# RWKV-7 recurrence: the solve of the triangle as a step of its own two units ahead, and inner products on quarters of the array

## Chip, cores and metric

The kernel runs on one core of one Trainium2 chip. The metric is the device time of one execution in microseconds; several runs are taken, and their median counts. Engines are called PE (TensorE), PEld (its weight loads), DVE (VectorE), ACT (ScalarE), POOL (GpSimd) and SP (SyncE, which here only issues DMAs).

## What is computed

A decoder trunk for 1024 tokens of width 1024: one layer with an RWKV-7 time mix and an MLP, then one layer with sliding-window attention and an MLP. What matters here is the time mix. After projections of the shifted input (r, k, v, decay w, rate a, gate g), a recurrence runs over the tokens for 16 heads of width 64, each with a 64x64 state S:

```python
def step(S, inp):
    r_t, w_t, k_t, v_t, a_t, b_t = inp
    sa = jnp.einsum('bhvk,bhk->bhv', S, a_t)
    S = S * w_t[:, :, None, :] + sa[..., None] * b_t[:, :, None, :] + v_t[..., None] * k_t[:, :, None, :]
    y = jnp.einsum('bhvk,bhk->bhv', S, r_t)
    return S, y
...
y = wkv7(rh, wh, kh, vh, -kk, kk * ah)
```

Then each head's y is normalised, a bonus term is added, the gate is applied, and an output product follows. All inputs and the output are float32.

## The kernel before

**Chunks and units.** The recurrence is not run token by token. Tokens go in chunks of L = 64. Inside a chunk the step is a triangular system: with the products of b and k with a and r (64x64 per head, masked), a unit lower triangle is inverted, and everything else is matrix products. A *unit* is 128 tokens (NC = 2 chunks) of 8 heads (GH; GP = 4 pairs of heads, one head of a pair on partitions 0 to 63, the other on 64 to 127). There are 16 units, in order of time, two groups of heads for each block of tokens.

**Steps of a unit.**
- `prep` (L574) loads `ld` (r, k, w, a of the unit, written by the projections to HBM), and makes RA (r and a, scaled), bk (b and k, scaled), EL (the chunk's decay) and bonus.
- `inner` (L627) multiplies bk by RA: for each of 8 (pair, chunk) and each half `hp` one product with K = 64, 128 columns and N = 128 (L642), four per PSUM tile and half. Of the result a quarter is copied to XT (ACT, L646), and two parts go through a mask to AR (L647) and RT (L648) on DVE. The diagonal 32x32 blocks of the triangle are stored to HBM (dXs, L659, issued on ACT's queue) and loaded as Xs with one block per partition (L661, SP). bk is transposed to BK (L665, L666).
- `solve` (L669) inverts the 32x32 blocks on POOL, 31 steps of two instructions (L680, L682) on TT, stores TT (dTT, L684), clears a block of RT with a memset on POOL (L687) and loads the inverse into RT (L689). The store and the loads are on SP's queue.
- `join` (L693) joins two 32x32 inverses to one of 64x64: a transpose on DVE (L700), two sets of small matmuls (L705, L711), copies on ACT (L707, L713).
- `chunks` (L716) runs the two chunks one after the other: L743, L745 (ACT), L748, L749, L752 (with RT, the inverse), L754 (DVE), L757, L759, L762 (DVE: the state for the second chunk, in SV), L763, L766, L767. bv is loaded and multiplied on POOL (L732).
- `finish` (L770) normalises y: L781 and L787 on PE, the power -1/2 on POOL (L791), `spread` (L563: the copy `wide` on ACT, L568, transposes L570), the gate, and the store of z.

**Order.** The Tile framework builds each engine's queue ahead of time: it walks the instructions by priority in a simulated time and puts each one on its engine's queue as soon as, in that time, its inputs and buffers are there. On the chip each engine works its queue in that order and waits where an input is late. `urgent` (L93) gives the recurrence one stream of priorities ahead of all else, in the order of the program. `recurrence` (L804) sets that order by strings: ORDER2 = 'cispfj' means chunks(n), inner(n+1), solve(n+1), prep(n+2), finish(n), join(n+1); ORDER0 and ORDER1 stand at the borders of the parts. The projections are made in three parts of 256, 256 and 512 tokens, so units 0 to 3, 4 to 7 and 8 to 15 need part 0, 1 and 2.

**Beside it.** Units 0 to 7 run beside the projections; then come the output product of the first 512 tokens (`mix_out`) and its MLP, beside which units 8 to 15 run. Projections and MLP split every weight and activation into two float32r halves, hi and lo: casts on ACT (L129), subtractions on DVE (L130), three matmuls each on PE (L134 to L136), weights loaded by SP (L269).

PSUM has pools `big` (4 banks: products), `sm` (2: prep and inner) and `sq` (2, `turn()`: join, chunks, finish).

Of the kernel before, what the change touches and what calls it, by code (L numbers as in the profile page):

```python
# [50 lines left out]


ORDER0 = 'cfipsj'
ORDER1 = 'cifpsj'
ORDER2 = 'cispfj'
# [19 lines left out]
class Trunk:  # L75
# [487 lines left out]
    def spread(self, src, ps):  # L563
# [3 lines left out]
        w = self.t(self.rp, "wide", [P, n, 2, D])  # L567
# [59 lines left out]
    def inner(self, prepared):  # L627
# [4 lines left out]
        AR = t("AR", [P, 2, GP * NC, 2 * L], 2)  # L632
        BK = t("BK", [P, GP * NC, 2, D], 2)
        RT = t("RT", [P, 2, GP * NC, L], 2)
# [15 lines left out]
        for hp in range(2):  # L650
            hs = self.sides(hp)[0]
            nc.sync.dma_start(AR[hs, hp], RA[hs])

# [6 lines left out]
        for js in range(JS):  # L660
            nc.sync.dma_start(Xs[js * 2 * NQ:(js + 1) * 2 * NQ], dX.rearrange("b h q k i -> (b h q) k i"))  # L661
        for r0 in range(0, GP, 2):
# [4 lines left out]
        return AR, BK, RT, EL, bonus, XT, Xs  # L667

    def solve(self, made):  # L669
# [3 lines left out]
        AR, BK, RT, EL, bonus, XT, Xs = made  # L673
# [11 lines left out]
        for hp in range(2):  # L685
# [5 lines left out]
        return made  # L691

    def join(self, made):  # L693

        nc = self.nc
        AR, BK, RT, EL, bonus, XT, Xs = made
# [12 lines left out]
        for q in range(n):  # L709
            for hp, b, k in sides:  # L710
                nc.tensor.matmul(ps[k:k + B, q], AT[k + B:k + L, q], RT[k + B:k + L, hp, q, B:], start=True, stop=True)  # L711
        for hp, b, k in sides:
            nc.scalar.copy(RT[k:k + B, hp, :, B:], ps[k:k + B, 0:n])  # L713
        return AR, BK, RT, EL, bonus

    def chunks(self, blk, g, made):  # L716
# [15 lines left out]
        nc.gpsimd.tensor_tensor(bv[L:], bv[L:], bonus[L:].unsqueeze(3).broadcast_to([L, NC, GH, D]), ALU.mult)  # L732
# [6 lines left out]
        for c in range(NC):  # L739
# [11 lines left out]
            for pi, hp, bs, ks in heads:  # L751
                nc.tensor.matmul(ps[bs, pi], RT[ks, hp, pi * NC + c], pb[ks, pi], start=True, stop=True)  # L752
# [5 lines left out]
            sn = t("sn", [P, GP, D])  # L758
# [360 lines left out]
```

## Time and profile before

| what | us |
|---|---|
| median of 3 runs (2684.1 to 2687.0) | 2686.05 |
| the profiled execution | 2683.85 |
| its span on the core | 2682.1 |
| PE busy in the span | 2549.6 |
| DVE busy | 1688.0 |
| ACT busy | 1289.1 |
| POOL busy | 616.9 |
| mean granted clock of PE, as a share of 2.4 GHz | 0.974 |

The profile is of one execution. Busy times are the time in which an engine had an instruction under way; matmuls are pipelined, so PE's busy time is not time at its peak. A clock below 1 means that for part of the stretch the lower of two levels was granted. In the profile L-numbers are lines of the kernel, "x16" is a count, "<-" names the tile written and those read, and in brackets stands how long the engine was idle before and who released it.

### The profile page before, as it was taken

Reading aid. Unit: us, or ns where it says so; the run is one execution under the profiler, and the core shown is the slowest. Engines: PE = TensorE matmul, PEld = TensorE weight load, DVE = VectorE, ACT = ScalarE, POOL = GpSimd, SP = SyncE. Lnnn points to the kernel's source line nnn. Section 1 sums busy time; section 2 is a strip of 40 time slices with the busy share of each in tenths; the row PEclk is TensorE's granted clock in tenths of the full one; section 3 lists DMA queues with packets and bytes.
Section 4 is the critical chain, followed back from the end, with each engine's and each line's share of the span. In section 5 each row is a group of like instructions: output and inputs, shape, how many; then the busy total and the mean of one; then the engine's idle time right before and its main releaser. Section 6 shows DMA issues by size and latency. Waiting matters only on the chain.

```text
span 2682.1 us, 43180 instructions
## 1 busy us (share of the span) xinstructions
PE 2549.6 (95%) x15226; PEld 2066.2 (77%) x15226; DVE 1688.0 (63%) x3204; ACT 1289.1 (48%) x2670; POOL 616.9 (23%) x1213
## 2 busy tenths in 40 slices
PE   7978988998889999999999999999999999999999
PEld 5867766765767777778888888888888888888887
DVE  8678788665766666545467876445899544444444
ACT  5555566455444434334455555334666433434342
POOL 6276643741464444410010000001000000000000
PEclk9988989999889999999999999999999999999999
DMA  5756644654634444333434444342446332423332
GB/s 178 203 171 171 181 115 121 181 145 148 178 101 117 121 117 117 109 103 119 142 94 150 123 129 146 92 154 90 136 142 204 114 102 91 125 91 102 98 98 96
DMA packets 440633, 349.62 MB, mean 130 GB/s; under 512 B 97105, under 2 KB 360417, under 8 KB 440417
## 3 DMA queue, kind: packets, MB, share of 16 engines
q1 hardware_dynamic: 423008, 344.77, 42.5%
q10 hardware_dynamic: 17408, 2.10, 0.5%
q8 instruction: 120, 1.97, 0.3%
q14 instruction: 97, 0.79, 0.1%
HBM read 280.71 MB, written 57.67 MB: 126 GB/s over the span
## 4 chain that ended last, share of the span: by engine, by line
PE 54%; DVE 2%; DMA 0%; ACT 0%; issue 0%; POOL 0%; DVEq 0%; ACTq 0%; POOLq 0%
PE big L134 17%; PE big L135 17%; PE big L136 17%; PE sm L134 1%; PE sm L135 0%; PE sm L136 0%; PE sq L956 0%; PE sq L957 0%; PE big L252 0%; DVE sc L962 0%; DVE wl L130 0%; DVE m2k L260 0%; PE sq L933 0%; DMA wr<-in_b_wq 0%; DVE b L1038 0%; DVE st L966 0%
## 5 line engine op out<-in xcount | busy, mean ns | idle before, releaser
L129 ACT CAST wh<-wr 128x512 fp32r<-128x512 f32 x741 | 458.2, 620 | 872.4 <-PE big L136 457.5
L130 DVE TENSOR_TENSOR wl<-wr,wh 128x512 fp32r<-128x512 f32 x741 | 529.4, 718 | 485.5 <-issue 226.0
L135 PE MATMUL big<-wl,m2k 128*128 128x512 f32 (+1 forms) x1472 | 580.6, 395 | 7.2 <-DVE wl L130 5.4
L134 PE MATMUL big<-m2k,wh 128*128 128x512 f32 (+3 forms) x1528 | 576.4, 380 | 9.8 <-ACT m2k L129 4.8
L136 PE MATMUL big<-m2k,wl 128*128 128x512 f32 (+2 forms) x1528 | 571.3, 376 | 7.4 <-DVE wl L130 7.3
L135 PE MATMUL big<-m2k,wh 128*128 128x512 f32 (+2 forms) x1528 | 571.1, 375 | 7.3 <-POOL m2k L130 4.2
L136 PE MATMUL big<-wh,m2k 128*128 128x512 f32 (+1 forms) x1472 | 567.5, 392 | 2.8 <-POOL m2k L130 2.8
L134 PE MATMUL big<-wh,m2k 128*128 128x512 f32 (+1 forms) x1472 | 515.9, 395 | 9.8 <-ACT m2k L129 7.5
L134 PEld LDWEIGHTS big<-m2k,wh 128*128 128x128 f32 (+1 forms) x1528 | 290.3, 190 | 70.8 <-ACT m2k L129 6.9
L136 PEld LDWEIGHTS big<-m2k,wl 128*128 128x128 f32 (+1 forms) x1528 | 290.8, 191 | 59.6 <-DVE wl L130 10.1
L134 PEld LDWEIGHTS big<-wh,m2k 128*128 128x128 f32 x1472 | 281.3, 192 | 71.1 <-ACT m2k L129 9.2
L135 PEld LDWEIGHTS big<-m2k,wh 128*128 128x128 f32 (+1 forms) x1528 | 290.6, 190 | 58.5 <-POOL m2k L130 6.7
L135 PEld LDWEIGHTS big<-wl,m2k 128*128 128x128 f32 x1472 | 282.1, 192 | 69.2 <-DVE wl L130 10.4
L136 PEld LDWEIGHTS big<-wh,m2k 128*128 128x128 f32 x1472 | 281.2, 191 | 59.3 <-POOL m2k L130 3.3
L680 POOL TENSOR_TENSOR tmp<-Xs,TT 128x60 f32<-128x60 f32 (+24 forms) x496 | 193.6, 390 | 142.0 <-DMA Xs<-dXs 105.4
L130 DVE TENSOR_TENSOR m2k<-relu,m2k 128x512 fp32r<-128x512 f32 (+1 forms) x200 | 137.0, 687 | 122.7 <-ACT m2k L129 122.0
L682 POOL TENSOR_TENSOR TT<-TT,tmp 128x60 f32<-128x60 f32 (+24 forms) x496 | 199.1, 401 | 37.8
L129 ACT CAST m2k<-relu 128x512 fp32r<-128x512 f32 (+1 forms) x272 | 146.4, 544 | 46.3 <-DVE relu L353 33.8
L322 DVE TENSOR_TENSOR b<-b,big 128x512 f32<-128x512 f32 x192 | 124.8, 681 | 10.2 <-PE big L136 9.7
L223 POOL TENSOR_TENSOR ss<-ss,mhalf 128x4 f32<-128x4 f32 (+1 forms) x10 | 8.9, 888 | 488.7 <-DVE ss L222 488.7
L223 POOL TENSOR_TENSOR qn<-qn,mhalf 128x8 f32<-128x8 f32 x16 | 26.7, 1671 | 399.3 <-DVE qn L222 346.0
L314 ACT ACTIVATE relu<-relu 128x512 f32<-128x512 f32 x128 | 80.8, 632 | 3.5
(229 smaller groups left out, 3089.7 us busy)
## 6 DMA issues: line engine op xcount, KB each, us to landing
wr<-in_mlp_w SPq DMA_DIRECT2D x512, 256.0 KB, 2.7
wr<-in_a_w_rkv SPq DMA_DIRECT2D x144, 256.0 KB, 3.1
ld<-dP SPq DMA_DIRECT2D x16, 1024.0 KB, 7.7
dS<-sc SPq DMA_DIRECT2D x28, 512.0 KB, 2.9
row<-dS SPq DMA_DIRECT2D x112, 128.0 KB, 2.8
dP<-stg SPq DMA_DIRECT2D x64, 128.0 KB, 2.8
AR<-RA SPq DMA_DIRECT2D x32, 256.0 KB, 4.5
Xs<-dXs SPq DMA_DIRECT2D x64, 128.0 KB, 2.7
```

Source lines behind the costliest of these rows:

```text
L129: self.nc.scalar.copy(hi, src)
L130: (engine or self.nc.vector).tensor_tensor(lo, src, hi.bitcast(F32), ALU.subtract)
L134: mm(ps, ah, bh, start=start, stop=False)
L135: mm(ps, ah, bl, start=False, stop=False)
L136: mm(ps, al, bh, start=False, stop=stop)
L223: nc.gpsimd.tensor_tensor(dst, dst, self.mhalf[:, :n], ALU.pow)
L314: nc.scalar.activation(r, r, AF.Square)
L322: nc.vector.tensor_tensor(v, v, ps[tt], ALU.add)
L680: nc.gpsimd.tensor_tensor(v, Xs[:, k:k + 1, k + 1:].broadcast_to([P, m, n]), TT[:, 0:m, k:k + 1].broadcast_to([P, m, n]), ALU.mult)
L682: nc.gpsimd.tensor_tensor(TT[:, 0:m, k + 1:], TT[:, 0:m, k + 1:], v, ALU.add)
```

## The change

The triangle of the inner products (b with a, the quarter that is solved) is made in a function of its own, `triangle`, which also stores and loads the blocks and runs `solve`, up to the store of dTT. `recurrence` calls it with `prep` in `begin(n + 3)`, after finish(n); `inner(n + 2)` stands before finish(n), and `join(n + 1)` before that. `inner` makes the remaining products, with 64 columns each: one set with N = 64 for RT (one mask instruction over 128 partitions instead of four over 64) and one with N = 128 for AR. RT's second half now holds the inverse for both halves of the heads. The memset and the loads of the inverse move from `solve` to `join`. Three short POOL instructions (memset, bv, the power) get a priority ahead of the stream. `finish` uses buffers of its own for the gate and the spread; `sn` shares pb's buffer and AT lies in XT.

```diff
-ORDER0 = 'cfipsj'
-ORDER1 = 'cifpsj'
-ORDER2 = 'cispfj'
...
-    def urgent(self, stream):
+    def urgent(self, stream, rank=1):
-        at = self.ahead.get(stream, -URGENT)
+        at = self.ahead.get(stream, -rank * URGENT)
...
-    def inner(self, prepared):
+    def triangle(self, prepared):
...
-        n = 2 * NC
-        for r0 in range(0, GP * NC, n):
-            pg = [self.small().rearrange("p (i m) -> p i m", i=n) for _ in range(2)]
-            for i in range(n):
-                for hp in range(2):
-                    hs = self.sides(hp)[0]
-                    nc.tensor.matmul(pg[hp][:, i], bk[hs, r0 + i], RA[hs, r0 + i], start=True, stop=True)
+        ps = self.small().rearrange("p (i m) -> p i m", m=L)
+        for i in range(GP * NC):
             for hp in range(2):
                 hs, bs, ks = self.sides(hp)
-                to = slice(r0, r0 + n)
-                nc.scalar.copy(XT[bs, to], pg[hp][bs, :, L:])
-                nc.vector.tensor_tensor(AR[ks, hp, to], pg[hp][ks], self.maskg[ks].unsqueeze(1).broadcast_to([L, n, 2 * L]), ALU.mult)
-                nc.vector.tensor_tensor(RT[bs, hp, to], pg[hp][bs, :, 0:L], self.maskg[bs, 0:L].unsqueeze(1).broadcast_to([L, n, L]),
-                                        ALU.mult)
...
+                nc.tensor.matmul(ps[bs, i], bk[hs, i, bs], RA[hs, i, L:], start=True, stop=True)
+        nc.scalar.copy(XT, ps)
...
+        return XT, self.solve(Xs)
+
+    def inner(self, prepared, tri):
...
+        for hp in range(2):
+            hs = self.sides(hp)[0]
+            nc.sync.dma_start(AR[hs, hp], RA[hs])
+        ps = self.small().rearrange("p (i m) -> p i m", m=L)
+        for i in range(GP * NC):
+            for hp in range(2):
+                hs, bs, ks = self.sides(hp)
+                nc.tensor.matmul(ps[bs, i], bk[hs, i, bs], RA[hs, i, 0:L], start=True, stop=True)
+        nc.vector.tensor_tensor(RT[:, 0], ps, self.maskg[:, 0:L].unsqueeze(1).broadcast_to([P, GP * NC, L]), ALU.mult)
+        n = GP * NC // 2
+        for r0 in (0, n):
+            ps = self.small().rearrange("p (i m) -> p i m", i=n)
+            for i in range(n):
+                for hp in range(2):
+                    hs, bs, ks = self.sides(hp)
+                    nc.tensor.matmul(ps[ks, i], bk[hs, r0 + i, ks], RA[hs, r0 + i], start=True, stop=True)
+            for hp in range(2):
+                ks = self.sides(hp)[2]
+                nc.vector.tensor_tensor(AR[ks, hp, r0:r0 + n], ps[ks], self.maskg[ks].unsqueeze(1).broadcast_to([L, n, 2 * L]), ALU.mult)
...
+    def join(self, made):
...
         for hp in range(2):
             r = self.sides(hp)[2].start
-            nc.gpsimd.memset(RT[r + B:r + L, hp, :, 0:B], 0.0)
+            with self.urgent("pool", 2):
+                nc.gpsimd.memset(RT[r + B:r + L, 1, :, 0:B], 0.0)
             for b in range(2):
-                nc.sync.dma_start(RT[r + b * B:r + (b + 1) * B, hp, :, b * B:(b + 1) * B],
+                nc.sync.dma_start(RT[r + b * B:r + (b + 1) * B, 1, :, b * B:(b + 1) * B],
                                   dT[:, :, b, hp].rearrange("j s q i -> (j s) q i"))
...
-            nc.vector.transpose(XT[b:b + B, :, 0:B], RT[k:k + B, hp, :, 0:B])
-        AT = self.t(self.rp, "AT", [P, n, B], F32)
+            nc.vector.transpose(XT[b:b + B, :, 0:B], RT[k:k + B, 1, :, 0:B])
+
+        AT = XT[:, :, 0:B]
...
+        with self.urgent("pool", 2):
+            nc.gpsimd.tensor_tensor(bv[L:], bv[L:], bonus[L:].unsqueeze(3).broadcast_to([L, NC, GH, D]), ALU.mult)
...
-            sn = t("sn", [P, GP, D])
+            sn = t("pb", [P, GP, D])
...
-        gt = t("m1", [P, GP, TB])
+        gt = t("gt", [P, GP, TB])
...
-        nc.gpsimd.tensor_tensor(r2, r2, self.mhalf[:, :GH], ALU.pow)
-        nc.vector.tensor_tensor(z2, z2, self.spread(rs, self.turn()), ALU.mult)
+        with self.urgent("pool", 2):
+            nc.gpsimd.tensor_tensor(r2, r2, self.mhalf[:, :GH], ALU.pow)
+        nc.vector.tensor_tensor(z2, z2, self.spread(rs, self.turn(), "wide2"), ALU.mult)
...
+        def begin(m):
+            if m < len(units):
+                ready[m] = self.prep(*units[m])
+                tri[m] = self.triangle(ready[m])
+
+        def inner(m):
+            if m < len(units):
+                made[m] = self.inner(ready.pop(m), tri.pop(m))
+
         with self.urgent("rec"):
-            made = self.inner(self.prep(*units[0]))
-            ready = self.prep(*units[1])
-            made = self.join(self.solve(made))
...
+            begin(0)
+            inner(0)
+            begin(1)
+            joined = self.join(made.pop(0))
+            inner(1)
+            begin(2)
         for n, u in enumerate(units):
             with self.urgent("rec"):
...
+                y, bv = self.chunks(*u, joined)
+                if n + 1 < len(units):
+                    joined = self.join(made.pop(n + 1))
+                inner(n + 2)
+                self.finish(*u, y, bv)
+                begin(n + 3)
             yield
```

## Rows read from the trace of the kernel before

**Rows 1.** Page, busy time of each engine: us (share of the span) xinstructions.
```profile
PE 2549.6 (95%) x15226; PEld 2066.2 (77%) x15226; DVE 1688.0 (63%) x3204; ACT 1289.1 (48%) x2670; POOL 616.9 (23%) x1213
```

**Rows 2.** Busy time by stage: stretch, length, engines, PE's granted clock, DMA share, GB/s.
```profile
120.00:700.00 580.00, 510.01 (x4151) 394.60 (x4150) 419.40 (x829) 326.20 (x723) 288.45 (x574) 0.93 0.54 158
700.00:820.00 120.00, 108.05 (x821) 87.92 (x822) 86.13 (x160) 48.60 (x95) 72.79 (x180) 0.86 0.43 118
820.00:1160.00 340.00, 324.83 (x2560) 258.26 (x2561) 215.55 (x396) 135.61 (x264) 150.67 (x349) 0.98 0.41 112
...
1260.00:2682.00 1422.00, 1411.24 (x6498) 1169.83 (x6496) 828.93 (x1577) 669.12 (x1359) 40.72 (x32) 1.00 0.39 121
```

**Rows 3.** Waits of DVE, 120 to 1260 us: in total, times, longest.
```profile
DVE XT L700 <- DMA RT<-dTT: 80.1, 17, 8.2
```

**Rows 4.** Timeline, 1019 to 1030 us: start, us, engine, line [idle before, releaser].
```profile
1021.95 0.38 SPq L684 DMA_DIRECT2D dTT<-TT  x1
...
1026.34 0.43 DVE L700 STREAM_TRANSPOSE XT<-RT 32x256 f32<-32x256 f32 x1 [7.51 <-DMA RT<-dTT]
...
1027.32 1.42 PE L743 MATMUL sq<-SV,AR 128*64 128x64 f32 x15 [3.19 <-issue]
```

**Rows 5.** Timeline of POOL in the MLP stage.
```profile
975.06 0.65 POOL L687 MEMSET RT<- 32x256 f32 x2 [17.10 <-PE sq L766]
987.92 2.14 POOL L791 TENSOR_TENSOR rs<-rs,mhalf 128x8 f32<-128x8 f32 x1 [12.21 <-DVE rs L790]
...
1041.41 0.65 POOL L687 MEMSET RT<- 32x256 f32 x2 [16.66 <-PE sq L766]
```

**Rows 6.** Groups by line, whole span: busy us, mean ns | idle before.
```profile
L682 POOL TENSOR_TENSOR TT<-TT,tmp 128x60 f32<-128x60 f32 (+24 forms) x496 | 199.1, 401 | 37.8
L680 POOL TENSOR_TENSOR tmp<-Xs,TT 128x60 f32<-128x60 f32 (+24 forms) x496 | 193.6, 390 | 142.0 <-DMA Xs<-dXs 105.4
```

**Rows 7.** Stretches round the waits of L700: two, then sums of ten and six.
```profile
423.00:439.00 16.00, 11.05 (x113) 8.31 (x111) 13.28 (x31) 10.03 (x22) 1.85 (x6) 0.89 0.52 154
...
741.00:757.00 16.00, 11.59 (x76) 9.33 (x75) 7.66 (x15) 1.97 (x4) 7.99 (x25) 0.69 0.52 133
...
886.00:902.00 16.00, 13.69 (x95) 10.67 (x92) 9.14 (x18) 4.68 (x9) 2.44 (x10) 0.89 0.39 99
...
sum 160.00, PE 135.92 PEld 105.84 DVE 103.98 ACT 77.02 POOL 45.88; mean PE 13.59 PEld 10.58 DVE 10.40 ACT 7.70 POOL 4.59
...
sum 96.00, PE 81.53 PEld 63.35 DVE 51.94 ACT 24.64 POOL 15.61; mean PE 13.59 PEld 10.56 DVE 8.66 ACT 4.11 POOL 2.60
```

**Rows 8.** Waits of PE: in total, times, longest.
```profile
PE sq L743 <- issue: 12.8, 6, 3.2
...
PE sq L705 <- DVE XT L700: 8.9, 3, 4.4
```

**Rows 9.** PE's products: chain that ended last, PE's timeline, group of L642.
```profile
1163.21 0.61 PE sq L752 x16
...
1173.00 0.86 PE sq L781 x2
...
946.64 1.16 PE L642 MATMUL sm<-RA,bk 64*128 64x128 f32 x16
947.74 0.50 PE L136 MATMUL big<-m2k,wl 128*128 128x512 f32 x1
...
L642 PE MATMUL sm<-RA,bk 64*128 64x128 f32 x512 | 56.5, 293 | 6.7 <-DVE RT L648 4.8 <-ACT wh L129 1.8
```

**Rows 10.** Groups by line on DVE and ACT.
```profile
L322 DVE TENSOR_TENSOR b<-b,big 128x512 f32<-128x512 f32 x192 | 124.8, 681 | 10.2 <-PE big L136 9.7
...
L648 DVE TENSOR_TENSOR RT<-sm,maskg 64x256 f32<-64x256 f32 x64 | 27.0, 422 | 1.1
...
L646 ACT COPY XT<-sm 64x256 f32<-64x256 f32 x64 | 23.4, 366 | 28.6 <-PE sm L642 26.3 <-PE sq L748 0.9 <-ACT XT L646 0.8
...
L666 ACT COPY BK<-sm 128x512 f32<-128x512 f32 x32 | 18.1, 588 | 5.8 <-PE sm L665 5.8
```

**Rows 11.** Waits of SP's queue, 820 to 1160 us.
```profile
SPq L684 <- POOL TT L682: 51.1, 6, 10.1
```

**Rows 12.** Waits of ACT.
```profile
ACT wide L568 <- POOL rs L791: 24.8, 12, 5.8
```

More of the change, by code (lines that the diff above doesn't have):

```diff
@@ L561, in project, with spread @@
         return nxt, self.gate_out(pt)
-    def spread(self, src, ps):
+    def spread(self, src, ps, tag="wide"):
         nc = self.nc
         n = src.shape[1]
-        w = self.t(self.rp, "wide", [P, n, 2, D])
+        w = self.t(self.rp, tag, [P, n, 2, D])
         nc.scalar.copy(w, src.unsqueeze(3).broadcast_to([P, n, 2, D]))
@@ L661, in inner @@
             nc.sync.dma_start(Xs[js * 2 * NQ:(js + 1) * 2 * NQ], dX.rearrange("b h q k i -> (b h q) k i"))
+        return XT, self.solve(Xs)
+    def inner(self, prepared, tri):
+        nc = self.nc
+        t = lambda tag, shape, bufs=1, dt=F32: self.t(self.rp, tag, shape, dt, bufs)
+        RA, bk, EL, bonus = prepared
+        AR = t("AR", [P, 2, GP * NC, 2 * L], 2)
+        BK = t("BK", [P, GP * NC, 2, D], 2)
+        RT = t("RT", [P, 2, GP * NC, L], 2)
+        for hp in range(2):
[17 more added lines that the diff above has]
+                nc.vector.tensor_tensor(AR[ks, hp, r0:r0 + n], ps[ks], self.maskg[ks].unsqueeze(1).broadcast_to([L, n, 2 * L]), ALU.mult)
         for r0 in range(0, GP, 2):
@@ L666, in inner, with solve @@
             nc.scalar.copy(BK[:, r0 * NC:(r0 + 2) * NC].rearrange("p i h d -> p (i h d)"), ps.rearrange("p i m -> p (i m)"))
-        return AR, BK, RT, EL, bonus, XT, Xs
-    def solve(self, made):
+        return AR, BK, RT, EL, bonus, *tri
+    def solve(self, Xs):
         nc = self.nc
         t = lambda tag, shape, bufs=1, dt=F32: self.t(self.rp, tag, shape, dt, bufs)
-        AR, BK, RT, EL, bonus, XT, Xs = made
         TT = t("TT", [P, B // JS, B])
@@ L684, in solve @@
         nc.sync.dma_start(dT.rearrange("j s b h q i -> (s b h q) j i"), TT)
+        return dT
+    def join(self, made):
+        nc = self.nc
+        AR, BK, RT, EL, bonus, XT, dT = made
         for hp in range(2):
             r = self.sides(hp)[2].start
-            nc.gpsimd.memset(RT[r + B:r + L, hp, :, 0:B], 0.0)
+            with self.urgent("pool", 2):
+                nc.gpsimd.memset(RT[r + B:r + L, 1, :, 0:B], 0.0)
             for b in range(2):
-                nc.sync.dma_start(RT[r + b * B:r + (b + 1) * B, hp, :, b * B:(b + 1) * B],
+                nc.sync.dma_start(RT[r + b * B:r + (b + 1) * B, 1, :, b * B:(b + 1) * B],
                                   dT[:, :, b, hp].rearrange("j s q i -> (j s) q i"))
[L691 to L696, printed above, removed]
         n = NQ // 2
@@ L710, in join @@
             for hp, b, k in sides:
-                nc.tensor.matmul(ps[k:k + B, q], AT[k + B:k + L, q], RT[k + B:k + L, hp, q, B:], start=True, stop=True)
+                nc.tensor.matmul(ps[k:k + B, q], AT[k + B:k + L, q], RT[k + B:k + L, 1, q, B:], start=True, stop=True)
         for hp, b, k in sides:
-            nc.scalar.copy(RT[k:k + B, hp, :, B:], ps[k:k + B, 0:n])
+            nc.scalar.copy(RT[k:k + B, 1, :, B:], ps[k:k + B, 0:n])
         return AR, BK, RT, EL, bonus
@@ L751, in chunks @@
             for pi, hp, bs, ks in heads:
-                nc.tensor.matmul(ps[bs, pi], RT[ks, hp, pi * NC + c], pb[ks, pi], start=True, stop=True)
+                nc.tensor.matmul(ps[bs, pi], RT[ks, 1, pi * NC + c], pb[ks, pi], start=True, stop=True)
             for hp, bs, ks in sides:
@@ L765, in chunks @@
             for pi, hp, bs, ks in heads:
-                nc.tensor.matmul(py[bs, pi], SV[bs, c, hp, pi], RT[bs, hp, pi * NC + c], start=True, stop=True)
+                nc.tensor.matmul(py[bs, pi], SV[bs, c, hp, pi], RT[bs, 0, pi * NC + c], start=True, stop=True)
             nc.vector.tensor_tensor(y[:, :, c], y[:, :, c], py, ALU.add)
@@ L806, in recurrence @@
         units = [(b, g) for b in range(T // TB) for g in range(NG)]
-        with self.urgent("rec"):
-            made = self.inner(self.prep(*units[0]))
-            ready = self.prep(*units[1])
-            made = self.join(self.solve(made))
-        part = lambda n: PART[units[min(n, len(units) - 1)][0]][0]
+        ready, tri, made = {}, {}, {}
+        def begin(m):
[5 more added lines that the diff above has]
+                made[m] = self.inner(ready.pop(m), tri.pop(m))
+        with self.urgent("rec"):
+            begin(0)
[4 more added lines that the diff above has]
+            begin(2)
         for n, u in enumerate(units):
             with self.urgent("rec"):
-                late = part(n + 1) != part(n)
-                order = ORDER0 if late else ORDER1 if part(n + 2) != part(n) else ORDER2
-                for what in order:
-                    if what == 'c':
-                        y, bv = self.chunks(*u, made)
-                    elif what == 'f':
-                        self.finish(*u, y, bv)
-                    elif n + 1 < len(units):
-                        if what == 'i':
-                            nxt = self.inner(ready)
-                        elif what == 's':
-                            nxt = self.solve(nxt)
-                        elif what == 'j':
-                            made = self.join(nxt)
-                        elif what == 'p' and n + 2 < len(units):
-                            ready = self.prep(*units[n + 2])
+                y, bv = self.chunks(*u, joined)
[4 more added lines that the diff above has]
+                begin(n + 3)
             yield
```

7 lines of the change are left out of this document (removed).

## The prediction

> **What bounds the kernel now.** I read the page's busy times first: TensorE (PE) is busy 95% of the span, every other compute engine 63% or less [rows 1]. Then the span by stage [rows 2]. From 1260 us on PE has 1411 of 1422 us at full clock: nothing to win there, and the change does not touch it. What can move lies between 120 and 1160 us, where the recurrence runs beside the projections and the first MLP. There PE sits idle 580.0-510.0 = 70 us, 120.0-108.1 = 12 us and 340.0-324.8 = 15 us, and the granted clock of 0.93, 0.86 and 0.98 is a mixture of the 2.4 and the 1.2 GHz level that costs another 0.07x580 = 41, 0.14x120 = 17 and 0.02x340 = 7 us. So 162 us is all that a better order can give, and whatever is added to PE's work after 700 us is paid nearly in full.
>
> Third, DVE's waits: in the recurrence the largest is L700, join's transpose, on the load of the solved triangle: 80 us in 17 waits [rows 3]. The timeline of one unit shows what stands behind it [rows 4]. POOL has ended the solve when its store is issued at 1021.95; with the load back it is 1026.34 before DVE, after 7.51 us at L700, goes on. Behind L700 queue L762, which makes the SV of the second chunk, and the wl halves of the MLP weights. PE waits 3.19 us for that SV. So unit n's second chunk waits for unit n+1's solve. POOL closes the circle [rows 5]: its memset for the next unit waits 17.10 us for the last read of RT, and the power for finish another 12.21, before the next solve starts at 987.92+2.14 = 990.06; that one is stored at 1021.95, 32 us later. Chunk, finish, solve, load and chunk again make a period of 1041.41-975.06 = 66 us, in which POOL stands for some 30.
>
> **The change part by part, against the profiled execution** (2683.85 us; the median of the runs, 2686.05, is 2 us above it, and the sum is laid on the median).
>
> *The solve two units ahead.* It is issued in begin(n+3) after finish(n) and first used in join(n+3), some two units later. POOL's solve work is (193.6+199.1)/16 = 24.5 us a unit [rows 6], well under a period, so the triangle should have landed long before L700, and the circle opens. What this frees I bound with stretches of 16 us round each wait of L700 [rows 7]. The six from 822 us on hold 96-81.5 = 14.5 us of idle PE, and four of them stand at a clock of 0.89 like the one shown, 4x0.11x16 = 7 us; at least the 12.8 us that PE waited before L743 [rows 8] are the stall's own. I take 20 of 21.5: **-20**. The ten earlier ones hold 24 of idle time, and 16 by their clocks (0.69 at 741 us the lowest). Two of them, at 423 and 741 us, belong to units 4 and 8, the first of a part: their rows come late from the projection, so the lead is lost there and what these two hold, 5+2 and 4+5, stays. At least the 8.9 us before L705 [rows 8] go. I take **-20**, near the 24 that is left. Late next, at these two units, is the load of ld, which nothing here moves.
>
> *Quarters.* Before, a unit had 16 products with K=64, 128 columns and N=128; each is two instructions in the trace. After, it has three sets of 32 instructions: two with 64 columns and N=64, one with 64 columns and N=128. The first two have the form of L752, 64x64 quarters on crossed halves into one bank: 16 in 0.61 us [rows 9], so 1.22 us a set. No row shows a quarter with N=128; nearest is L642 itself where the two row halves alternate: 16 in 947.74-946.64 = 1.10 us, so 2.20. Below that lies L781, 0.86 us for two of 512 columns, so 107 ns for 128, and halved for two at once 1.7 us a set; above lies twice L752, 2.5. The sum is 4.64 us a unit. Before, L642 keeps PE 56.5 us; its 45 bursts each reach some 0.06 us past the start of the next matmul (1.16 against 1.10), which leaves 54, 3.4 a unit. The change adds 1.26 us x 16 = 20 us (bounds 12 and 25), with 1024 matmuls and as many weight loads more. Up to 700 us the 12% of idle time can take some of it, and I leave that out: **+20**.
>
> The Trainium skill (TensorEngine Tiling (Array Packing), Restrictions and Gotchas) speaks against this: different row tiles are to write different PSUM banks and cannot access the same one at once. L752 writes one bank from both row halves and takes 38 ns, where 64 columns alone need 53 by L781, so here the rule is not seen; with it the sum would be that of rival 4.
>
> *DVE and ACT.* The mask over RT was four instructions of 422 ns and becomes one of 128x512, for which L322's 681 is nearest; AR keeps its four. DVE loses 1.0 us a unit. ACT copied XT in four of 366 and does it in one of 588: 0.9 less [rows 10]. After 700 us this hides behind PE; before, DVE is busy 72% and feeds PE. **-3**, between 0 and -8, all that DVE saves in the eight units before 700, and nearer the lower half because ACT and POOL feed PE too.
>
> *Moves.* memset, bv and the power go ahead of the solve on POOL; wide2, gt, pb and XT only part or share buffers. The DMAs are the same in number: on SP 4 loads of Xs, one store of dTT, 4 loads of RT and 2 of AR a unit, on ACT 4 of dX. The loads of RT go from solve to join, no longer right behind the store; AR goes ahead of the products. SP's wait for POOL before the store of dTT, 51.1 us in six [rows 11], stays; what queues behind it are weight loads. The recurrence, no longer held by its circle, gets ahead: 66 less the 7 of the wait is a period near 59 us. Unit 7 then ends earlier and the wait before mix_out shrinks: **-6**, between 0 and -20 (two thirds of the 29 us lost from 700 to 820 us). New waits that the other order brings: **+5**, between 0 and +40, the size of what goes.
>
> **Sum** -20-20+20-3-6+5 = **-24**: 2686-24 = **2662 us**, with 2640 to 2680 for this case.
>
> **Rivals.**
> 1. *POOL's lag moves to finish; slower.* SP's wait says that POOL ends each solve 51.1/6 = 8.5 us later than the order of the queues supposes. Now the solve lies beside chunk and finish, and the power (L791) and bv stand between its steps. If they come late, ACT stands at wide, with the casts of the weights behind it, PE's L570 waits, and the stall is back in a new place. At the 20/6 = 3.4 us that one costs PE now, in 14 units, +48: 2686-40+48+20-3 = 2711. For it: the lag is in the rows. Against it: POOL has 30 us of slack a unit and its short work goes first. It decides from a delay above the 5.8 us that wide has already waited for the power once, 24.8 us in twelve waits [rows 12].
> 2. *An even trade.* Only the waits that PE names go (12.8+8.9 = 22) and the quarters cost 20: 2684, no change.
> 3. *The circle was the brake of the whole stage.* All 61 us round the stalls go, with -20 and -8 from the ranges above and +20 for the quarters: 2617. For it: beside PE, DVE is the busiest engine up to 700 us, and it is DVE that stands at L700.
> 4. *Quarters do not overlap in one bank; slower.* Each instruction then takes its time alone: 32x(53+53+107) ns = 6.8 us a unit, 109 in all against 54: +55 instead of +20, 2697. Only N=64 is seen to overlap in one bank. It is the Trainium skill's rule named above.
> 5. *The solve is not ahead.* TT, Xs and RA have one buffer each, so triangle and solve may be held until join needs them: L700 waits as today and the quarters cost 20: 2703. Against it: the solve needs 32 of the 59 us.
>
> **How the numbers follow.** Chances: forecast 0.46, rival 1 0.19, rival 2 0.11, rival 3 0.15, rival 4 0.05, rival 5 0.04. A measurement of this kernel can tell 0.2%, some 5 us, from no change. Faster: the forecast nearly whole, rival 3 and a little of rival 2, 0.62. Same: most of rival 2 and the forecast's edge, 0.10. Slower: rivals 1, 4 and 5, 0.28. The range runs from the middle of rival 3 to that of rival 1: 2618 to 2711.
>
> **What would show it.** Right: L700's waits on the load of RT under 20 us in sum; POOL's memset no longer waiting for L766; PE's waits before L743 gone; a period near 59 us beside the MLP; 74 us of PE for the three new sets; a clock of 0.99 from 820 to 1160. Wrong: ACT's wide waiting for POOL over 80 us in sum (rival 1); 53 and 107 ns an instruction for the quarters (rival 4); L700 still at 80 us (rival 5).

## The result, and the profile after

The changed kernel takes **2760.3 us** (median of 4 runs, 2756.2 to 2768.8); the kernel before, on the same chip, 2685.9. The ratio is **1.0282**, 95% interval 1.0257 to 1.0307: slower by 76 us, above the range, where 24 us less was forecast. Below, differences in us are ratios times 2686, since each run has its own runs of the kernel before beside it.

The page's busy times, then the span by stage (columns as in [rows 1] and [rows 2]):

```profile
PE 2579.6 (94%) x16250; PEld 2085.8 (76%) x16250; DVE 1655.4 (60%) x3156; ACT 1277.6 (46%) x2622; POOL 605.5 (22%) x1213
...
120.00:700.00 580.00, 500.71 (x4550) 387.79 (x4551) 389.46 (x772) 306.55 (x674) 281.57 (x570) 0.92 0.51 147
700.00:820.00 120.00, 81.51 (x837) 64.95 (x837) 69.47 (x137) 32.81 (x62) 74.47 (x182) 0.76 0.44 121
820.00:1160.00 340.00, 314.06 (x2790) 245.67 (x2783) 197.39 (x376) 127.06 (x245) 143.98 (x352) 0.95 0.40 109
```

The profiled execution's span is 2758.3 us, 76 more than before. PE is busy 30 us longer and idle 178.7 against 132.5, 46 more. So two thirds of the loss are waits. The stage that fell most is 700 to 820 us: PE is busy 81.5 of 120 us at a clock of 0.76, where [rows 2] have 108.1 at 0.86.

Now the waits, by engine (total, times, longest), against [rows 3, 8, 11, 12]. The last line is of the kernel before, finish's spread there:

```profile
DVE XT L710 <- DMA RT<-dTT: 57.8, 18, 9.7
...
DVE ld L580 <- DMA ld<-dP: 40.6, 13, 6.5
...
PE sq L565 <- ACT wide L563: 33.9, 8, 8.6
...
PE sq L716 <- DVE XT L710: 9.6, 1, 9.6
...
SPq L693 <- POOL TT L691: 62.9, 6, 13.4
...
ACT wide L563 <- POOL rs L804: 40.9, 13, 12.3
...
PE sq L570 <- ACT wide L568: 1.1, 2, 0.9
```

The wait for the solved triangle (L710, L700 before) has shrunk by 22 of 80 us only, and PE waits for it as long as before (9.6 us against 8.9). PE's wait of 12.8 us before L743 is gone (L755 now), but finish's spread (L565) has 33.9 us where it had 1.1. And in the groups by line, the three sets of inner products:

```profile
L668 PE MATMUL sm<-RA,bk 64*64 64x128 f32 x512 | 37.9, 288 | 5.1 <-DVE RT L661 2.2 <-DVE AR L671 2.1 <-ACT XT L633 0.8
...
L632 PE MATMUL sm<-RA,bk 64*64 64x64 f32 x512 | 25.4, 241 | 0.4 <-DVE bk L604 0.3
...
L660 PE MATMUL sm<-RA,bk 64*64 64x64 f32 x512 | 24.6, 241 | 3.1 <-DVE bonus L614 3.1
```

Together 87.9 us against the 56.5 of [rows 9].

The timelines of PE and SP between 650 and 800 us show the stage that fell; the last line is the same load (L838) in the kernel before:

```profile
654.12 0.68 PE L778 MATMUL sq<-RT,SV 64*64 64x64 f32 x16
761.33 0.31 PE L716 MATMUL sq<-XT 32*32 32x32 f32 x2 [9.58 <-DVE XT L710]
763.87 1.06 PE L716 MATMUL sq<-XT 32*32 32x32 f32 x30
766.76 2.08 PE L793 MATMUL sq<-y,center 128*128 128x512 f32 x2
...
785.40 0.39 SPq L815 DMA_DIRECT2D dZ<-z  x1
787.75 1.30 SPq L853 DMA_DIRECT2D stg<-dZ  x3
...
696.32 1.27 SPq L838 DMA_DIRECT2D stg<-dZ  x3
```

Unit 7's chunks are done at 655, but its finish (L793) runs at 767: in PE's queue it stands behind join(8) (L716), which needs the triangle of unit 8, whose rows the projection of part 2 has only just made. The mixing product of the first half reads unit 7's dZ, and its loads (stg) that need it go out 91 us later than in the kernel before. That made the first theory: **the border** between parts 1 and 2 is the loss.

### The profile page after: what moved, and what is told of

Read it like the earlier page. It is cut to its first block, busy times and chain, and to the rows that moved or that the text cites. A ratio compares the mean times of both kernels' runs of the same rounds, so it can differ in the third digit from the quotient of the medians.

```text
span 2758.3 us, 45108 instructions
## 1 busy us (share of the span) xinstructions
PE 2579.6 (94%) x16250; PEld 2085.8 (76%) x16250; DVE 1655.4 (60%) x3156; ACT 1277.6 (46%) x2622; POOL 605.5 (22%) x1213
## 3 DMA queue, kind: packets, MB, share of 16 engines
q1 hardware_dynamic: 423008, 344.77, 40.9%
## 4 chain that ended last, share of the span: by engine, by line
PE 76%; POOL 9%; DMA 6%; DVE 4%; issue 2%; ACT 2%; SPq 1%; ACTq 0%; DVEq 0%; POOLq 0%
PE big L129 22%; PE big L130 22%; PE big L131 22%; POOL TT L691 4%; POOL tmp L689 4%; DMA ld<-dP 2%; DMA Xs<-dXs 1%; DVE wl L125 1%; DVE relu L348 1%; DMA stg<-dZ 1%; PE sq L755 1%; DMA dP<-stg 1%; PE sq L764 1%; PE sq L769 1%; PE sm L129 1%
## 5 line engine op out<-in xcount | busy, mean ns | idle before, releaser
L130 PE MATMUL big<-m2k,wh 128*128 128x512 f32 (+3 forms) x1528 | 569.8, 374 | 16.5 <-DVE m2k L125 9.3
L129 PE MATMUL big<-m2k,wh 128*128 128x512 f32 (+3 forms) x1528 | 572.1, 378 | 8.7 <-ACT m2k L124 4.5
L130 PEld LDWEIGHTS big<-m2k,wh 128*128 128x128 f32 (+2 forms) x1528 | 289.7, 190 | 69.9 <-POOL m2k L125 10.6
L129 PEld LDWEIGHTS big<-m2k,wh 128*128 128x128 f32 (+2 forms) x1528 | 289.1, 190 | 70.0 <-ACT m2k L124 7.1
L689 POOL TENSOR_TENSOR tmp<-Xs,TT 128x60 f32<-128x60 f32 (+24 forms) x496 | 184.9, 373 | 152.5 <-DMA Xs<-dXs 115.7
```

Of the source, the lines that this page charges most:

```text
L129: mm(ps, ah, bh, start=start, stop=False)
L130: mm(ps, ah, bl, start=False, stop=False)
L689: nc.gpsimd.tensor_tensor(v, Xs[:, k:k + 1, k + 1:].broadcast_to([P, m, n]), TT[:, 0:m, k:k + 1].broadcast_to([P, m, n]), ALU.mult)
```

## The experiments

**1. The border, and three mends of the order.** e1 puts finish first at a border, e4 in every unit, e6 adds to e1 a tile of its own for prep's w rows.

```diff
+    early = part(n + 1) != part(n)
+    if early:
+        self.finish(*u, y, bv)
     if n + 1 < len(units):
         joined = self.join(made.pop(n + 1))
     inner(n + 2)
-    self.finish(*u, y, bv)
+    if not early:
+        self.finish(*u, y, bv)
```

> The changed kernel with one edit: where the next unit lies in another part (units 3 and 7), finish(n) is emitted ahead of join(n+1) and inner(n+2). Theory border: finish(7) stands in TensorE's queue behind join(8), which waits for the rows of part 2; its dZ is stored at 785 instead of about 697 us, and the product that reads it starts late. TensorE's busy time times clock in 700 to 820 us was 108.05 x 0.86 = 92.9 before and 81.51 x 0.76 = 61.9 after, so 31 us come back: 2725 to 2735 us, and unit 7's dZ is stored before 710. Theory steady state: the loss is the new stall inside every unit (spread of finish behind ACT, 33.9 us in 8), and the stretch 700 to 820 only shows it piled up: within 8 us of 2760. Theory quarters: the inner products themselves: within 8 us of 2760.

Measured: 2737.8 us, 1.0183 (1.0165 to 1.0200), 27 us less than the changed kernel. Unit 7's dZ is stored at 678.7, and the stage has 93.2 busy at 0.87. The border is a real cost, a third of the loss; 49 us are left.

> The changed kernel with finish(n) directly behind chunks(n) in every unit, join(n+1) and inner(n+2) behind it. Theory border: gives back the same 31 us as the edit at the borders alone, 2720 to 2735, and more only if finish's sum of squares on VectorE no longer stands behind the first operation of the next prep, which waits for its load (5.4 us at 895): the spread's waits (33.9 us in 8) would fall to under 10 us, and the time to 2700 to 2715. Rival: join(n+1) behind finish comes too late for the chunks of n+1, a period of 65 us instead of 61, and 2740 to 2760.

2736.7 us, 1.0175 (1.0156 to 1.0194): 2 us below e1, within the noise, and PE's wait at finish's spread stays (20.3 us, 21.7 in e1; with prep's spread 25 in both). Finish first everywhere gives nothing more.

```diff
-    ld = t("ld", [P, 4, GP, TB])
-    nc.sync.dma_start(ld, self.dP[g][pt][:, :, :, t0:t0 + TB])
...
+    lw = t("lw", [P, GP, TB], 2)
+    nc.sync.dma_start(lw, self.dP[g][pt][:, 2, :, t0:t0 + TB])
+    ld = t("ld", [P, 3, GP, TB])
+    nc.sync.dma_start(ld[:, 0:2], self.dP[g][pt][:, 0:2, :, t0:t0 + TB])
+    nc.sync.dma_start(ld[:, 2], self.dP[g][pt][:, 3, :, t0:t0 + TB])
...
-    z = t("z", [P, GP, TB], 2)
+    z = t("z", [P, GP, TB])
```

> The edit at the part borders, and the w rows of prep's load in a tile of their own with two buffers (three loads instead of one; z has one buffer instead of two to make room). Theory: in the steady state VectorE stands 5.2 to 5.4 us at prep's first operation for the load of ld, with finish's variance queued behind it, and TensorE then waits for the spread (33.9 us in 8 in the changed kernel). With w there early, VectorE's wait for that load falls from 40.6 us in 13 to under 10, the spread's from 33.9 to under 15, and the time is 15 to 25 us below that of the border edit alone: 2700 to 2720. Rival: POOL's own queue holds the power of finish (its waits for the L778 ending, 39.5 us in 4), and the load only happened to be there: within 6 us of the border edit alone.

2729.3 us, 1.0149 (1.0134 to 1.0165), 9 below e1. VectorE's wait for w falls to 15.3 us, but it now waits for the next rows that prep reads (26.8 us in 14 at the product with a), and finish's spread keeps 18.5 of 21.7. A small gain, not the cause.

**2. The quarters alone, in the kernel before.**

```diff
-    pg = [self.small().rearrange("p (i m) -> p i m", i=n) for _ in range(2)]
...
-            nc.tensor.matmul(pg[hp][:, i], bk[hs, r0 + i], RA[hs, r0 + i], start=True, stop=True)
...
+    nc.tensor.matmul(ps[bs, i], bk[hs, i, bs], RA[hs, i, L:], start=True, stop=True)
+    nc.scalar.copy(XT, ps)
...
+    nc.tensor.matmul(ps[bs, i], bk[hs, i, bs], RA[hs, i, 0:L], start=True, stop=True)
...
+    nc.tensor.matmul(ps[ks, i], bk[hs, r0 + i, ks], RA[hs, r0 + i], start=True, stop=True)
```

> The kernel before with its order of work, and of the change only the three sets of inner products on quarters of the array (64x64 quarters, one copy for the triangle, one mask for the second set, two for the third). My sum: the sets measure 25.4 + 24.6 + 37.9 = 87.9 us in the changed kernel against 56.5 before, and the recurrence is done at 1160 us, so 31 us of TensorE time at most, less what lies in its idle time: +15 to +30, 2701 to 2716. Theory quarters (they are the whole loss): 2745 to 2765. Rival (they are hidden in waits, the loss is all order): 2680 to 2695.

**2751.8 us, 1.0236 (1.0219 to 1.0253): +63.** My sum of +15 to +30 is out: the quarters alone cost most of the loss. PE is busy 23 us longer there, and idle 41 longer. So either array time costs double in this stage, or the quarters do something else. e10 adds array time and nothing else to the kernel before:

```diff
-    for i in range(n):
+    for i in [*range(n)] * (1 if r0 else 2):
```

> The kernel before; of each unit's inner products the first half (8 of 16 calls) is done twice into the same bank, with the same result. Nothing else is added: no eviction, no wait, no transfer. 256 calls take 56.5 us there, 0.221 us each, so 128 more are 28 us of TensorE time, about what the quarters add (87.9 - 56.5 = 31). Theory array: the stage pays this and nothing beside, 2710 to 2722. Theory amplified: with this much more in the recurrence its waits grow too, as with the quarters alone (idle time +41), and 2735 to 2755. Rival hidden: under 2700.

2706.6 us, 1.0083 (1.0065 to 1.0101): the products are busy 26.5 us longer (83.0 against 56.5 us in the group of L642), and that costs 22. Array time is paid nearly once, not twice. The sets of e2 are busy 86.0 us, 29.5 more than before; at this rate about 25 of the 63 us are that, an estimate. For the rest, look at unit 9 of e2, on POOL, ACT and PE:

```profile
890.04 0.21 POOL L688 TENSOR_TENSOR tmp<-Xs,TT 128x8 f32<-128x8 f32 x1
890.21 1.65 POOL L799 TENSOR_TENSOR rs<-rs,mhalf 128x8 f32<-128x8 f32 x1
...
891.88 0.62 ACT L568 COPY wide<-rs 128x512 f32<-128x512 f32 x1 [10.78 <-POOL rs L799]
...
892.56 1.12 PE L570 MATMUL sq<-ident,wide 128*128 128x128 f32 x4 [5.72 <-ACT wide L568]
```

and at unit 10 of the kernel before, where POOL's steady order shows:

```profile
908.18 0.65 POOL L687 MEMSET RT<- 32x256 f32 x2 [16.58 <-PE sq L766]
921.05 2.14 POOL L791 TENSOR_TENSOR rs<-rs,mhalf 128x8 f32<-128x8 f32 x1 [12.21 <-DVE rs L790]
923.16 0.23 POOL L680 TENSOR_TENSOR tmp<-Xs,TT 128x31 f32<-128x31 f32 x1
```

In the kernel before, POOL takes the clearing and the power first and then the solve's 31 pairs of steps (from 128x31 to 128x8). With quarters the triangle's set comes first and is copied out of PSUM earlier, the planner puts the solve's steps earlier too, and the power stands behind all 31 (in other units of e2 behind 9 to 31). e20 puts it back in front:

```diff
     nc.gpsimd.tensor_copy(TT, self.eye)
+    if self.power is not None:
+        nc.gpsimd.tensor_copy(t("tmp", [P, 144])[:, 0:2], self.power)
...
+        self.power = rs[:, 0]
```

> The kernel before with the quarters alone, and one copy of two elements in front of the solve's steps that reads the power of the last finish: POOL then takes the power and the clearing of RT ahead of the steps, as in the kernel before, where in the quarters alone they stand behind 10 to 31 of them. Theory POOL's order: the quarters bring the triangle and so the solve earlier, finish's power falls behind the steps (10.8 us of ScalarE's wait at 881, 5.7 of TensorE's), and that is most of the 40 us beyond the array time: 2705 to 2720, the spread's waits 24 to under 8 us. Rival (the waits only change their names): 2740 to 2755.

2720.2 us, 1.0106 (1.0079 to 1.0133): 35 us less than e2, and ACT's wait for the power falls from 59.2 us to 6.1. So of the quarters' 63 us some 25 are array time, and 35 go away with **an order on POOL that they brought about**. That the order itself makes the 35 fits the waits, but the copy also makes the solve wait for the power and all queues are planned anew, so it is not shown. Is that order a fault of the kernel before as well?

> The kernel before with nothing of the change, and the copy that puts the power of the last finish in front of the solve's steps on POOL. In it three powers stand behind 15 to 31 steps and four clearings of RT behind 8 to 29, all in the first eight units; here the powers all stand in front. Theory POOL's order costs in any kernel: 10 to 25 us less than before, 2660 to 2677. Rival: the first eight units wait for the projection anyway, within 5 us of 2686; or the solve that starts later gives it back through VectorE's waits for RT (80.1 us), 2690 to 2705.

The same copy in the kernel before: 2703.6 us, 1.0070 (1.0053 to 1.0087), **19 us slower**. In front is not better everywhere: in the first eight units the solve then starts later (unit 3's at 346.05 instead of 318.42), which may be the reason. Two more edits of the kernel before, which add no work to speak of, say how much hangs on it:

> The kernel before with the one part of the change that is neither the move nor the quarters: POOL's clearing of RT, the bonus product and finish's power at a higher priority for the planner. POOL's order changes in the first eight units alone (two powers that stood behind 15 and 31 of the 31 steps now stand behind 14 and none). If that was a cost: 2670 to 2680. If not: within 4 us of 2685.

2691.0 us, 1.0002 (0.9990 to 1.0014): the priorities alone are nothing.

> The kernel before with one edit: the w rows of prep's load in a tile of their own with two buffers (z has one). VectorE's wait for that load is 22.6 us in 11 there. If this wait is a cost in any order of the work: 8 to 15 us less, 2672 to 2682. If it only costs where finish's variance stands behind it (spread's waits in the kernel before are 4.8 us in all): within 5 us of 2687.

2696.5 us, 1.0043 (1.0029 to 1.0056): slower by 12, with two loads more a unit and nothing else added. So an edit that hardly adds work can move this kernel by 12 to 19 us, and differences of that size between two runs need not have the cause that the edit was made for.

**3. The move without the quarters.** The old product in two halves with N=64 each, over all 128 weight columns: k with the triangle, r in inner.

```diff
+    AK = t("AK", [P, 2, GP * NC, L], 3)
...
+    nc.tensor.matmul(ps[:, i], bk[hs, i], RA[hs, 1, i], start=True, stop=True)
...
+    nc.tensor.matmul(ps[:, i], bk[hs, i], RA[hs, 0, i], start=True, stop=True)
```

> The order of the border edit with the triangle in its own step two units ahead, but no quarters: the step multiplies the k half of RA by both halves of bk over the full height (64 columns), which gives the triangle and the k half of AR (AR is kept as two tiles, the k half with three buffers), and inner multiplies the r half in the same way. Array time of the products as in the kernel before, 56.5 us instead of 87.9. Room is made by one buffer for z and by finish's spread in prep's tile. Theory quarters cost their array time and the waits beside it (quarters alone +63 us): 2737.8 less 31 to 63, 2675 to 2707. Rival (the loss of the quarters alone was a planned order that came out badly, not their time): 2725 to 2745.

**2844.8 us, 1.0593 (1.0572 to 1.0615).** The groups by line of e13, then one of its bursts at full clock, and for comparison one of quarters with N=64 in the changed kernel:

```profile
L662 PE MATMUL sm<-RA,bk 64*128 64x64 f32 x512 | 89.9, 348 | 10.4 <-DVE AK L636 10.3
L634 PE MATMUL sm<-RA,bk 64*128 64x64 f32 x512 | 64.3, 305 | 0.6 <-DVE bk L604 0.5
...
780.95 3.39 PE L634 MATMUL sm<-RA,bk 64*128 64x64 f32 x32
...
890.19 1.10 PE L660 MATMUL sm<-RA,bk 64*64 64x64 f32 x32
```

My expectation took half of N for half the time; 154 us came out instead of 56.5. The single records of the traces say why. In the burst at 780.95 most instructions start 0.111 us apart, although N is 64. In the kernel before (L642 at 946.64, N=128) they start in pairs, one on each row half 6 to 8 ns apart, and in the run of the burst a pair every 0.111 us. So on one row half the smaller N saves nothing, and there are twice as many instructions; and e13's loop finishes one row half before the other, so that they no longer run side by side. This run doesn't separate the move from the quarters: it adds this cost of its own. It does say why the quarters are the cheap way to make the triangle alone: at 890.19 they start in pairs too, and a pair every 0.058 us.

**4. What the solve costs, before and after the move.** The 31 pairs of steps left out:

```diff
-    for k in range(B - 1):
+    for k in range(0):
```

> The kernel before with the solve's 31 pairs of steps left out (the inverse is then the identity; the load, the copy of the identity and the store of TT stay). It bounds from above what a solve two units ahead can ever give: POOL's chain is gone, so VectorE's waits for RT (80.1 us in 17) are gone too. The sum had 20 + 6 us for it, so 2655 to 2665 by the sum; if the circle was the brake of the whole stage, 2600 to 2630; if these waits lie beside other work, above 2675.

> The kernel with the border edit, with the same steps left out. If the solve two units ahead is off the path, as the change means it to be, within 8 us of 2737.8. If POOL's queue (finish's power behind the steps of the solve) is what the spread's waits come from, 2700 to 2725, and the spread's waits (25 us) under 8.

The kernel before: 2628.3 us, 0.9771 (0.9750 to 0.9791), **61 us less**. The moved kernel: 2675.5 us, 0.9950 (0.9929 to 0.9971), **63 less than e1**. This is the answer to the prediction's main step: the steps cost the same two units ahead as one. It says a second thing: without any steps the moved kernel is still 48 us above the kernel before without steps, as e1 is 49 above the kernel before. So the loss that is left in e1 is there without any step on POOL too, and without work that waits behind the steps.

Where do the 63 us lie? PE's busy time and clock by stretch, of e1 and then e15:

```profile
120.00:650.00 530.00, 457.22 (x4372) 0.92 0.52 149
650.00:880.00 230.00, 184.34 (x1543) 0.87 0.43 123
880.00:1260.00 380.00, 372.99 (x3097) 0.97 0.39 111
...
120.00:650.00 530.00, 481.78 (x4546) 0.94 0.53 154
650.00:880.00 230.00, 202.05 (x1994) 0.91 0.50 142
880.00:1260.00 380.00, 379.21 (x2772) 1.00 0.37 110
```

By the prediction's measure, idle time and the clock's share, e1 loses 35, 27 and 18 us more than e15 in the three stretches. That is 80 where the time has 63, so these are shares rather than sums, but most of it lies before 880 us, and some in the steady part too. POOL in e1, first and last step of units 8, 9 and 10:

```profile
734.14 1.39 POOL L689 TENSOR_TENSOR tmp<-Xs,TT 128x31 f32<-128x31 f32 x1 [21.19 <-DMA Xs<-dXs]
763.18 0.21 POOL L689 TENSOR_TENSOR tmp<-Xs,TT 128x8 f32<-128x8 f32 x1
768.76 0.24 POOL L689 TENSOR_TENSOR tmp<-Xs,TT 128x31 f32<-128x31 f32 x1 [2.21 <-DMA Xs<-dXs]
796.50 0.21 POOL L689 TENSOR_TENSOR tmp<-Xs,TT 128x8 f32<-128x8 f32 x1
802.19 0.24 POOL L689 TENSOR_TENSOR tmp<-Xs,TT 128x31 f32<-128x31 f32 x1 [2.35 <-DMA Xs<-dXs]
832.57 0.21 POOL L689 TENSOR_TENSOR tmp<-Xs,TT 128x8 f32<-128x8 f32 x1
```

Three solves of 28 to 31 us run end to end once the rows of part 2 are there, and whatever else POOL has to do queues among them. PE's first product of unit 8's chunks in the kernel before, e1 and e15:

```profile
758.88 0.69 PE L743 MATMUL sq<-SV,AR 128*64 128x64 f32 x16
```

```profile
783.49 0.69 PE L755 MATMUL sq<-SV,AR 128*64 128x64 f32 x16
```

```profile
708.04 0.69 PE L755 MATMUL sq<-SV,AR 128*64 128x64 f32 x16
```

Two runs tried to name the way in which the steps cost.

```diff
-    with self.urgent("pool", 2):
-        nc.gpsimd.tensor_tensor(r2, r2, self.mhalf[:, :GH], ALU.pow)
```

> The kernel with the border edit, with finish's power left out (z is scaled by the variance instead of its root's inverse), the solve's steps all there. Leaving the steps out gave 62 us. If they cost by holding the power back: the spread's waits (25 us in TensorE's queue) fall under 5 and the time to 2695 to 2715. If they cost by RT coming late and by the late half of the queue (VectorE, the triangle): 2725 to 2740.

2735.4 us, 1.0187 (1.0168 to 1.0207): no gain. PE's wait at the spread, 25 us in e1, falls to 4 (nearly all of it prep's), and PE's idle time as a whole hardly falls (2735.0-2576.3 = 158.7 us of the span, 162.4 in e1). So the most conspicuous new wait of the changed kernel is a symptom, at least once the border is mended.

> The changed kernel with all three mends together: finish first at the part borders, w early, and the copy in front of the solve's steps. Here the copy waits for a power one unit older, so five powers still stand behind 9 to 31 steps; that is what two units ahead means on a queue that is taken in order. Theory: so it changes little, 2720 to 2735 (2729 without the copy), and stays above the kernel before. Rival: the copy gives here what it gave the quarters alone (31 us): 2695 to 2705.

2726.2 us, 1.0161 (1.0140 to 1.0182): as the theory had it, little: no better than e6, whose ratio is 1.0149. These two are the best of the moved kernels, 40 and 43 us above the kernel before.

The last two move the steps to another engine, in the kernel before: e27 in the first unit of each part, e28 in all sixteen.

```diff
-    nc.gpsimd.tensor_copy(TT, self.eye)
+    eng.tensor_copy(TT, self.eye)
...
-    nxt = self.solve(nxt)
+    nxt = self.solve(nxt, self.nc.vector if late else self.nc.gpsimd)
```

> The kernel before; the solve's steps of the first unit of each part (units 0, 4 and 8) run on VectorE instead of POOL, the other thirteen stay. There the solve can't be ahead, since the part's rows have just come: unit 8's steps take POOL from 714.8 to 743.1 us, and its chunks start at 758.9 (708 with the steps left out). VectorE's operations of such sizes take 0.16 (128x8) to 0.42 us (128x256), so 62 of them some 15 us, 13 us sooner at three places. Theory that the steps' 61 us lie mostly where a part begins: 10 to 30 us less than before, 2655 to 2677. Rival: VectorE holds the weights' split back by as much (lo of each weight tile is its work), within 6 us of 2686.

> The same with the steps of all sixteen units on VectorE: POOL's queue has no steps that the power, the clearing or the bonus could stand behind. VectorE gets 16 times 15, 240 us more in the first 1260. Theory that POOL's slow steps are the cost and VectorE has room (63% of the span): 2640 to 2670. Rival: VectorE becomes the engine that the weight stream waits for, above 2700.

2692.7 us, 1.0039 (1.0025 to 1.0053), and 2698.2 us, 1.0061 (1.0040 to 1.0081): neither beats the kernel before. For the place of the 61 us e27 is no test: unit 8's steps are 0.16 to 0.24 us each on DVE, but they stand among the weight splits and last from 701.57 to 745.58, 44 us where POOL took 28. So that the steps cost mostly at the parts' beginnings is a reading of the traces, not what a run has shown; what would take them off there is open.

## Why the prediction was wrong

Forecast and measurement lie 100 us apart: 43 of them are the quarters' term (+63 by e2, +20 forecast), 33 the moves' (+27 by e1, -6 forecast), 26 the solve's (-14 by e1 against e2, -40 forecast).

*What bounds the kernel* held: the loss lies before 1260 us; from 1160 to 1260 us PE is busy 100.0 of 100 us at full clock in both kernels, and after that it is idle for 10 and 11 us.

*The solve two units ahead, -20 and -20: the step that failed.* It said that the triangle would have landed long before L700, because the solve's 24.5 us fit in a period, and took the idle time round L700's waits for the gain. L700's waits fell to 57.8 us, not under 20, and in e1, with the border mended, they are 75.8. PE's wait before chunk went, the one before join did not. What the step had wrong shows in unit 14 of e1, on POOL, SP, DVE and PE:

```profile
1058.95 0.21 POOL L691 TENSOR_TENSOR TT<-TT,tmp 128x8 f32<-128x8 f32 x1
1059.19 0.37 SPq L693 DMA_DIRECT2D dTT<-TT  x1
...
1065.61 0.43 DVE L710 STREAM_TRANSPOSE XT<-RT 32x256 f32<-32x256 f32 x1 [3.69 <-DMA RT<-dTT]
...
1144.30 0.69 PE L755 MATMUL sq<-SV,AR 128*64 128x64 f32 x16
```

The lead is there: the steps end 85 us before the unit's chunks (51 in the kernel before). But join's transpose has moved ahead with the solve: DVE stands for its load and takes it 6 us after the last step. From 870 to 1160 us, where the lead is whole, L710 waits 28.6 us in e1 and 14.5 in the changed kernel, L700 32.4 in the kernel before. So a longer lead does not by itself take this wait away. The two exceptions that the step granted, units 4 and 8, were half of the units: in e1 the steps of units 0 to 5, 8 and 9 end 18 to 44 us before the unit's chunks, those of the others 68 or more. e14 and e15 give the result in one figure, 61 us for the steps before and 63 after. The prediction's measure shows where the move wins and loses against e2, whose lines are:

```profile
120.00:650.00 530.00, 453.98 (x4284) 0.90 0.51 146
650.00:880.00 230.00, 193.00 (x1626) 0.91 0.47 135
880.00:1260.00 380.00, 357.29 (x3059) 0.96 0.38 106
```

Up to 650 us e1 loses 14 us less than e2, from 880 us on 20 less (18 against 38), but from 650 to 880 us, where part 2 begins, 18 more. So beside the quarters the first -20 came out, by this estimate from one profile each, and most of the second was lost again. In all the move, with the small parts of the change that e1 has and e2 has not, is worth 14 us, of the size of the 12 and 19 that e11 and e24 lost by little more than a new order.

*Quarters, +20: mis-sized.* At full clock the forms were right: 16 of the N=128 quarters take 1.09 us at 893.51 in the changed kernel, 1.10 had been taken. But the stage runs partly at half clock, and the three sets came to 87.9 us instead of 74: 87.9-56.5 = 31 us of array time, above the upper bound of 25; e10 prices it at some 25. What the sum had no term for is the other 38 of the 63: 35 of them go in e20, where the power stands in front of the steps on POOL. Whether they lie in POOL's order is open: without steps the power has nothing to stand behind, and e15 is still 48 us above e14. So in the moved kernel some 23 us beyond the array time have another cause, which no run names.

*The Trainium skill's rule* (TensorEngine Tiling (Array Packing), Restrictions and Gotchas), that row tiles can't access one bank at once, was not seen here at N=128 either: 68 ns an instruction (16 in 1.09 us at 893.51), where 107 was the price alone. Rival 4 is out.

*Moves, -6: wrong sign.* "Unit 7 then ends earlier and the wait before mix_out shrinks": its chunks did end at 655, but its finish was put behind join(8) in the program and so in PE's queue, and the wait grew; e1 prices it at 27. The rule that a wait added in a queue delays all that is behind it was applied to SP and POOL, not to PE. The period came nearly as forecast: from unit 9's power to unit 13's it is 61.0 us in the changed kernel (59 forecast), 66.2 before. But e2, without the move, has 63.1, and the time did not fall with it in either.

*Rival 1* (POOL's lag moves to finish) named the place and the sign: the spread's wait went from 1.1 us to 33.9. Its price was wrong: ACT's wait for the power is 40.9 us, under the 80 that was to decide, though its longest, 12.3, is above the 5.8 from which the rival was to come in; and e16 takes PE's part of it away for no gain. The loss came by another way. *Rival 3* had 61 us as what there is to win, and e14 measures 61 for the steps; the rival's figure was idle time and clock in stretches round the waits, so that the two agree may be luck. *Rival 5*, the solve not ahead, resembles the first units of each part, where the rows come late; its sign, L700's waits near 80 us, came in e1, but with the solve well ahead in half of the units. *DVE and ACT, -3*: the work did fall (1655 against 1688 us), and nothing shows it in the time.

The sum that the runs give instead: quarters +63 (some 25 array time), the move -14, the border +27, together +76. These are differences along one chain of runs, from the kernel before over e2 and e1 to the changed kernel, and the terms need not add up in another order.

## What to carry to other kernels

A lead of k units can pay only from the k-th unit after each restart, and only if what uses the result does not move ahead with it; before sizing it, count how many units run with the lead, and price the work by leaving it out before and after. When an edit changes when something becomes ready, read the new order of every in-order queue behind it, PE's too: a step moved ahead of another also holds it back. A wait that stands out in the profile is worth its length only if nothing is late right behind it; take it away alone before building on it.

## What the runs showed of the hardware

- Instructions of fp32 products with 64 rows at full clock, start to start on one row half: 0.111 us with 128 weight columns and N=128 (L642 before, 946.64), the same 0.111 with 128 weight columns and N=64 (e13, 780.95), 0.109 with 64 weight columns and N=128 (changed kernel, 893.51), 0.058 with 64 and N=64 (890.19). So N below 128 saved nothing unless the weight columns were halved too.
- Where the program alternates the two row halves, two such instructions start 6 to 8 ns apart and run side by side. e13, whose loop does not, and which has twice the instructions and lower clocks, took 154 us for its products where the kernel before took 56.5.
- In e13 the granted clock was lower than in the kernel before although PE was busy less: 98.7 of 120 us at 0.73 from 700 us on and 305.9 of 340 at 0.85 from 820 us on, against 108.1 at 0.86 and 324.8 at 0.98 [rows 2]. What of it comes from its products is not shown.

```profile
700.00:820.00 120.00, 98.67 (x553) 0.73 0.43 132
820.00:1160.00 340.00, 305.87 (x2462) 0.85 0.37 99
```

- The solve's steps of unit 8 take 0.16 to 0.24 us each on DVE (e27) and 0.21 to 1.25 on POOL in the kernel before, and still moving them there gained nothing.
